# How a turned page is cut into four transfers on its way to DRAM: 128 partitions by 256 columns instead of 32 partitions by 1024 columns

## The chip, the cores and the metric

One core of one Trainium2 chip runs the whole kernel. A core has a matrix engine (TensorE, PE in the profile), a vector engine (VectorE, DVE), a scalar engine (ScalarE, ACT), a general engine (GpSimd, POOL), a sequencer that only issues transfers here (SyncE, SP), and 16 DMA engines that carry transfers between DRAM and the on-chip buffer (SBUF, 128 partitions). The metric is the device time of one execution in microseconds (us); lower is better. Changes of less than 0.2% are taken as no change.

## The reference, cut to what matters

Two layers of an encoder with 256 tokens of width 4096. Each layer normalises, multiplies by one wide weight matrix (4096 x 11264), runs 16 attention heads and 8 bidirectional retention heads on the pieces, and multiplies back by 4096 x 4096:

```python
for l in range(DEPTH):                       # DEPTH = 2
    proj = rmsnorm(x, norm_w[l]) @ w_in[l]
    aq, ak, av, ag, rq, rk, rv, rg = jnp.split(proj, SPLIT_POINTS, axis=-1)
    aq = apply_axial_rope(rmsnorm(aq...), rope) * attn_scale
    ak = apply_axial_rope(rmsnorm(ak...), rope)
    a_out = jax.nn.silu(ag) * gqa_attention(aq, ak, av)
    r = bidirectional_retention(rope(rq), rope(rk) * ret_scale, rv, ...)
    r_out = jax.nn.silu(rg) * rmsnorm(r, ret_norm[l])
    x = x + jnp.concatenate([a_out, r_out], axis=-1) @ w_out[l]
return rmsnorm(x, final_norm)
```

All in float32. The kernel gets that precision by splitting each operand into a high and a low part and summing three products on PE.

## The kernel before, in words

**Weights.** The two weight matrices stream from DRAM in tiles of 128 x 1024 elements (512 KB). SP loads most of them (`wraw`); ACT casts each to its high part (`whi`), DVE subtracts to get the low part (`wlo`). Some groups use a seven-product scheme, for which DVE also forms sums of tiles (`wsum`). Every few tiles are "far": POOL loads the high part directly (`fhi`), ACT writes its negative into `flo`, and POOL then issues a second load of the same weights that is added onto `flo`. PE multiplies `whi`, `wlo`, `fhi`, `flo` by the activations (`x7h`, `x7l`, `x8h`, `x8l`) into eight PSUM banks (`M` in the profile).

**Side work.** Beside this stream, the results of each block become rotary queries and keys, gates, attention probabilities and retention weights. Small products of these go through one PSUM bank (`ps`) at places that are fixed between the weight products of PE's program.

**Turning.** A product often needs its operand with tokens and features exchanged. That is done in two halves. `turned` is one DVE instruction that transposes each 32 x 32 block of a page of 128 x 1024 elements, in place among the partitions. `store` then writes the page to a DRAM buffer with the blocks exchanged, in four transfers of 128 KB that POOL issues one after the other. A later transfer (`fetch`, or `Turn.fetch`, or the two loads of `retention_weights`) reads the buffer back as a whole. `store` is called for the turned keys (`k_dram`), queries (`q_dram`), gates (`g_dram`), attention probabilities (`p_dram`), retention queries and keys (`rq_dram`, `rk_dram`) and for the activations of the next matrix (`next_dram`).

In the buffer, element (row 32b + e, column 256a + f) comes from the page's partition 32a + e, column 256b + f, with a and b from 0 to 3, e from 0 to 31 and f from 0 to 255. A contiguous piece is therefore 256 elements, 1 KB, and a store has 512 of them.

**Who waits.** A fetch waits for all four transfers of its store. The page itself lies in one of nine shared buffers (`pg`); whatever is written next into that buffer waits for the four transfers too.

**What sets the order.** A model in the kernel (classes `Model` and `Rings`) plays the program while it is written and decides, engine by engine, the order of the instructions; the result is a fixed program. The model prices a transfer by `transfer`, from the length of its contiguous piece and the number of pieces. All instructions are issued from one recording helper, so nearly all have the line L458 in the profile, and tile names tell them apart.

Of the kernel before, what the change touches and what calls it, by code (L numbers as in the profile page):

```python
# [19 lines left out]
SEQ = 256  # L20
# [13 lines left out]
BLK = 32  # L34
# [490 lines left out]
def hybrid_encoder(  # L525
# [14 lines left out]
    ve, ac, pe, gp, sy = (  # L540
        Engine(e, engine, model, active)
        for e, engine in (("V", nc.vector), ("A", nc.scalar), ("P", nc.tensor), ("G", nc.gpsimd), ("S", nc.sync))
    )
# [39 lines left out]
    def drop(n=1):  # L583

        def dropped():
            held[0] -= n
            own(-n)

        do(dropped)
# [839 lines left out]

    def store(room, to):  # L1430

        to = to.rearrange("(b e) (a f) -> a e b f", e=BLK, a=4)
        for a in range(4):
            gp.dma_start(to[a], room[BLK * a : BLK * (a + 1), :].rearrange("e (b f) -> e b f", b=4))
        drop()

    def fetch(src, name):
# [48 lines left out]
    def rotary(v, L, kind, to):  # L1486
# [38 lines left out]
        drop()  # L1525
        yield
        store(v, to)
        return rs if kind == "aq" else None

# [15 lines left out]
    def attention_pair(g, h, kv, qT, rs, done):  # L1545
# [38 lines left out]
        drop()  # L1584
        yield
        store(room, p_dram[2 * (g % 2) + h // 2])
        yield

# [26 lines left out]
    def attention_group(L, g, gacc, qacc):  # L1615
        def gates():
            yield from gate(gacc, L)
            room = page([P, KG * SEQ], "room")
            turned(gacc, room)
            drop()  # L1620
            yield
            store(room, g_dram[g % 2])

        yield from gates()
        while "aq" not in L.tables:
            yield
        rs = yield from rotary(qacc, L, "aq", q_dram[g % 2])
        yield
        L.rs[g] = rs
# [701 lines left out]
```

## Time and profile before

| | |
|---|---|
| median of 3 runs | 2576.78 us (2576.16 to 2577.53) |
| the profiled execution's own time | 2576.86 us |
| its span in the profile | 2575.1 us |
| PE busy | 2562.3 us |
| DVE busy | 2374.0 us |
| ACT busy | 1706.2 us |
| POOL busy | 459.7 us |
| granted PE clock | 0.999 |

The span runs from the first to the last instruction of the program; 1.8 us of the execution lie outside it. PE is busy nearly all the time, but its busy time is no proof that it never waits, so its waits are read apart. "A <- B" in a list of waits says that A stood idle until B was done, with the total in us, the number of times and the longest. In a timeline each row has the start, the length, the engine, the operation, the tiles written and read, and in brackets the idle time before and what ended it. "POOL DMA_DIRECT2D" is the time in which POOL issues a transfer, not the time until it has landed.

### The profile page before, as it was taken

What the parts mean: (1) busy time and instruction counts of PE and PEld (TensorE: products, weight loads), DVE (VectorE), ACT (ScalarE), POOL (GpSimd) and SP (SyncE); (2) the same over time, 40 slices, a digit from 0 to 9 for tenths busy, and PEclk for the clock granted to TensorE, in tenths of its full rate; (3) what the DMA queues carried; (4) which work ended last, traced back from release to release, by engine and by line L of the source; (5) the groups of instructions that cost most, each with busy time, mean ns of one, the idle gap of its engine ahead of it and who ended that gap; (6) DMA issues with size and microseconds to landing.
All of it is one profiled execution on the core that took longest, in us unless ns stands there. A gap on an engine that the chain in (4) does not pass through costs nothing.

```text
span 2575.1 us, 34335 instructions
## 1 busy us (share of the span) xinstructions
PE 2562.3 (100%) x11482; PEld 2120.2 (82%) x11482; DVE 2374.0 (92%) x3001; ACT 1706.2 (66%) x2459; POOL 459.7 (18%) x676
## 2 busy tenths in 40 slices
PE   9999999999999999999999999999999999999998
PEld 6888888888888888888888888888888888888886
DVE  7999999999989999988999999999999899999887
ACT  7866676666655668665776666766666566776565
POOL 0111221211111111111221112212211112111111
PEclk9999999999999999999999999999999999999999
DMA  8988988988778787988998989888887887888986
GB/s 316 316 266 267 290 258 275 287 273 254 224 238 260 227 288 239 295 263 254 331 310 253 274 260 297 275 262 285 272 264 233 241 250 234 284 248 265 270 255 219
DMA packets 197969, 687.07 MB, mean 267 GB/s; under 512 B 24224, under 2 KB 24352, under 8 KB 197792
## 3 DMA queue, kind: packets, MB, share of 16 engines
q1 hardware_dynamic: 126592, 446.81, 49.1%
q0 software_dynamic: 71200, 238.07, 36.8%
q8 instruction: 90, 1.47, 0.2%
q14 instruction: 87, 0.71, 0.1%
HBM read 637.60 MB, written 47.19 MB: 266 GB/s over the span
## 4 chain that ended last, share of the span: by engine, by line
PE 98%; DMA 1%; DVE 0%; issue 0%; ACT 0%; POOL 0%; SPq 0%; POOLq 0%; DVEq 0%; ACTq 0%
PE M L458 94%; PE ps L458 4%; DMA q<-q_dram 0%; DMA full<-in_xT 0%; DVE wlo L458 0%; ACT full L458 0%; DVE cb L458 0%; SPq L458 0%; ACT whi L458 0%; ACT x7h L458 0%; DVE xf L458 0%; ACT pTh L458 0%; POOL last L458 0%; ACT ps L458 0%; DVE aql L458 0%
## 5 line engine op out<-in xcount | busy, mean ns | idle before, releaser
L458 ACT CAST whi<-wraw 128x1024 fp32r<-128x1024 f32 (+1 forms) x814 | 757.2, 936 | 336.0 <-PE M L458 289.8
L458 DVE TENSOR_TENSOR wlo<-wraw,whi 128x1024 fp32r<-128x1024 f32 (+1 forms) x814 | 869.6, 1077 | 47.5 <-ACT whi L458 43.8
L458 ACT CAST whi<-wsum 128x1024 fp32r<-128x1024 f32 x416 | 436.7, 1050 | 264.5 <-PE M L458 121.7
L458 DVE TENSOR_TENSOR wlo<-wsum,whi 128x1024 fp32r<-128x1024 f32 x416 | 507.3, 1220 | 91.1 <-ACT whi L458 61.1
L458 PE MATMUL M<-whi,x7h 128*128 128x512 f32 x1463 | 569.9, 390 | 0.0
L458 PE MATMUL M<-whi,x7l 128*128 128x512 f32 x1463 | 569.6, 389 | 0.0
L458 PE MATMUL M<-wlo,x7h 128*128 128x512 f32 x1463 | 475.0, 389 | 0.0
L458 PE MATMUL M<-whi,x8l 128*128 128x512 f32 x1165 | 453.6, 389 | 0.0
L458 PE MATMUL M<-whi,x8h 128*128 128x512 f32 x1165 | 453.6, 389 | 0.0
L458 PE MATMUL M<-wlo,x8h 128*128 128x512 f32 x1165 | 361.1, 389 | 0.0
L458 PEld LDWEIGHTS M<-wlo,x7h 128*128 128x128 f32 x1463 | 274.5, 188 | 57.6 <-DVE wlo L458 0.4
L458 PEld LDWEIGHTS M<-whi,x7h 128*128 128x128 f32 x1463 | 274.7, 188 | 56.8 <-DVE cb L458 0.4
L458 PEld LDWEIGHTS M<-whi,x7l 128*128 128x128 f32 x1463 | 274.7, 188 | 56.4 <-issue 0.2
L458 DVE TENSOR_TENSOR wsum<-wraw 128x1024 f32<-128x1024 f32 x208 | 253.6, 1219 | 4.2 <-DMA wraw<-in_w_out 1.6
L458 PEld LDWEIGHTS M<-wlo,x8h 128*128 128x128 f32 x1165 | 218.7, 188 | 45.6
L458 PEld LDWEIGHTS M<-whi,x8h 128*128 128x128 f32 x1165 | 218.7, 188 | 45.5 <-DVE ca L458 0.6
L458 PEld LDWEIGHTS M<-whi,x8l 128*128 128x128 f32 x1165 | 218.7, 188 | 45.3 <-DVE x8l L458 0.3
L458 ACT ACTIVATE flo<-fhi 128x1024 fp32r<-128x1024 f32 (+1 forms) x142 | 149.1, 1050 | 143.0 <-PE M L458 140.9
L458 PE MATMUL M<-whi,x 128*128 128x512 f32 x738 | 227.4, 389 | 0.0
L458 POOL DMA_DIRECT2D fhi<-in_w_in x104 | 58.0, 557 | 863.0 <-PE M L458 852.7
L458 PE MATMUL M<-fhi,x8l 128*128 128x512 f32 x417 | 162.4, 389 | 0.0
L458 PE MATMUL M<-fhi,x8h 128*128 128x512 f32 x417 | 162.3, 389 | 0.0
(287 smaller groups left out, 3197.9 us busy)
## 6 DMA issues: line engine op xcount, KB each, us to landing
wraw<-in_w_in SPq DMA_DIRECT2D x596, 512.0 KB, 5.7
wraw<-in_w_out SPq DMA_DIRECT2D x218, 512.0 KB, 6.1
fhi<-in_w_in POOLq DMA_DIRECT2D x104, 512.0 KB, 4.8
flo<-in_w_in POOLq DMA_DIRECT2D x104, 512.0 KB, 8.2
fhi<-in_w_out POOLq DMA_DIRECT2D x35, 512.0 KB, 4.8
flo<-in_w_out POOLq DMA_DIRECT2D x35, 512.0 KB, 8.5
full<-next_dram POOLq DMA_DIRECT2D x24, 512.0 KB, 8.7
p_dram<-room POOLq DMA_DIRECT2D x64, 128.0 KB, 5.3
```

The costliest lines, as they stand in the source:

```text
L458: op.call()
```

## The change

`store` still makes four transfers of 128 KB to the same places. Before, each took 32 partitions of the page with all their 1024 columns; now each takes all 128 partitions with 256 columns. The walk on the DRAM side was 32 rows (4 KB apart), in each of them four pieces 128 KB apart; now it is four pieces of a row (1 KB apart), for each of them 32 rows 4 KB apart.

```diff
     def store(room, to):
 
-        to = to.rearrange("(b e) (a f) -> a e b f", e=BLK, a=4)
-        for a in range(4):
-            gp.dma_start(to[a], room[BLK * a : BLK * (a + 1), :].rearrange("e (b f) -> e b f", b=4))
+        to = to.rearrange("(b e) (a f) -> b a e f", e=BLK, a=4)
+        for b in range(4):
+            gp.dma_start(to[b], room[:, b * SEQ : (b + 1) * SEQ])
         drop()
```

Piece length and piece count are the same (128 pieces of 1 KB in a transfer), so the model's price is the same, and every engine's instructions stand in the same order as before. Only the shape of the stores differs, in every one of them. Two places on POOL show it, with the shape on the DRAM side at the end of a row. The first is in layer 0, a store of turned queries and one of attention probabilities, and the fetch of these (before, then now):

```order
L458 DMA q_dram<-cb 32x4x256 x4
L458 DMA p_dram<-room 32x4x256 x2
L458 DMA fhi<-in_w_in 128x1024
L458 DMA p_dram<-room 32x4x256
L458 DMA flo<-in_w_in 128x1024
L458 DMA p_dram<-room 32x4x256
L458 DMA pT<-p_dram 128x1024
```

```order
L458 DMA q_dram<-cb 4x32x256 x4
L458 DMA p_dram<-room 4x32x256 x2
L458 DMA fhi<-in_w_in 128x1024
L458 DMA p_dram<-room 4x32x256
L458 DMA flo<-in_w_in 128x1024
L458 DMA p_dram<-room 4x32x256
L458 DMA pT<-p_dram 128x1024
```

Nothing moved; the transfers of a store count 4 x 32 rows of 256 elements instead of 32 x 4. The second is in layer 1, two stores of attention probabilities with the weight loads and the fetches around them (before, then now):

```order
L458 DMA p_dram<-room 32x4x256 x3
L458 DMA fhi<-in_w_in 128x1024
L458 DMA p_dram<-room 32x4x256
L458 DMA flo<-in_w_in 128x1024
L458 DMA sgT<-g_dram 128x1024
L458 DMA pT<-p_dram 128x1024
L458 DMA p_dram<-room 32x4x256 x4
```

```order
L458 DMA p_dram<-room 4x32x256 x3
L458 DMA fhi<-in_w_in 128x1024
L458 DMA p_dram<-room 4x32x256
L458 DMA flo<-in_w_in 128x1024
L458 DMA sgT<-g_dram 128x1024
L458 DMA pT<-p_dram 128x1024
L458 DMA p_dram<-room 4x32x256 x4
```

Here too a weight load stands between the third and the fourth transfer of a store, as before.

## The prediction

> **What bounds the kernel now.** I read the page's busy times first, then the list of PE's waits, since a busy PE alone proves nothing.
>
> ```profile
> span 2575.1 us, 34335 instructions
> PE 2562.3 (100%) x11482; PEld 2120.2 (82%) x11482; DVE 2374.0 (92%) x3001; ACT 1706.2 (66%) x2459; POOL 459.7 (18%) x676
> ...
> PE ps L458 <- DVE junk L458: 1.1, 1, 1.1
> PE M L458 <- DMA fhi<-in_w_in: 1.0, 2, 0.7
> PE M L458 <- ACT full L458: 0.2, 1, 0.2
> ```
>
> PE is the bound: it lacks 12.8 us of the span, and its waits on others sum to 2.3 us. The only wait on a transfer is 1.0 us, on a weight load. So no store of a turned page costs PE a visible moment today. A faster store can therefore give back 1.0 us at the very most, while a slower one can cost, if somewhere the slack between a store's landing and PE is thin. That asymmetry decides the forecast, so the rest of the reading is about slack. First the transfers themselves, from the list of issues, the queues, and the view of the tile `room`:
>
> ```profile
> q1 hardware_dynamic: 126592, 446.81, 49.1%
> q0 software_dynamic: 71200, 238.07, 36.8%
> p_dram<-room POOLq DMA_DIRECT2D x64, 128.0 KB, 5.3
> next_dram<-room POOLq DMA_DIRECT2D x64, 128.0 KB, 6.5
> L458 POOL DMA_DIRECT2D p_dram<-room x64: 552/574/912, 255.8 to 1835.1; - x64
> DMA to landing us min/median/max: 2.4/5.5/11.8
> DMA packets 197969, 687.07 MB, mean 267 GB/s; under 512 B 24224, under 2 KB 24352, under 8 KB 197792
> ```
>
> POOL's queue is q0, SP's is q1. Only 128 packets lie between 512 B and 2 KB, so the 1 KB pieces of the stores (512 in a page) do not travel as packets of their own; four share one of 4 KB. A transfer of a store takes POOL 0.574 us to issue and lands 2.4 us later when nothing is in its way, 5.5 us in the middle, 11.8 us at worst.
>
> Then who stands still until a store has landed, from the waits of POOL and of DVE:
>
> ```profile
> POOL pT L458 <- DMA p_dram<-room: 35.1, 5, 11.5
> POOL full L458 <- DMA next_dram<-room: 21.9, 4, 9.4
> POOL rkq L458 <- DMA rq_dram<-cb: 11.2, 3, 5.2
> POOL k L458 <- DMA k_dram<-ca: 5.9, 1, 5.9
> DVE pTl L458 <- DMA p_dram<-room: 1.8, 2, 1.1
> ```
>
> Thirteen times POOL holds a fetch, and all that is queued behind it, until the last transfer of a store is in. Twice DVE itself stops, because `pTl` is written into the buffer that a store is still reading. DVE is 92% busy, so time that it loses is not soon made up.
>
> **The change, part by part.**
>
> *POOL's instructions.* Four issues per store stay four, in the same order, with the same waits that matter. Their length should stay 0.574 us, since the pieces are as many (128). Should it depend on pieces per DMA engine instead, the nearest longer issue is that of `rkq`:
>
> ```profile
> L458 POOL DMA_DIRECT2D rkq<-rk_dram x8: 884/916/1067, 599.1 to 2149.5; - x8
> ```
>
> That is 0.34 us more, 1.0 us over the three issues ahead of a store's last. I take nothing, since the count of pieces is nearest to the store's own row, and keep 1.0 us for the upper end.
>
> *What carries a transfer.* Before, both sides of a transfer count 32 rows outermost; now the page's side counts 128 and the DRAM side 4. If the work is handed to DMA engines along the outermost count, a transfer that was spread over sixteen can now go to four. From q0's row: 36.8% of 16 x 2575.1 us is 15,162 us of engine time for 238.07 MB, so a packet of 4 KB takes 0.261 us. A transfer is 32 packets. On sixteen engines that is two each, 0.52 us; on four it is eight each, 2.09 us. No row decides between the two: no transfer of before has an outermost count so small. I hold four the likelier, because four rows to hand out cannot occupy sixteen engines unless the walk is cut through its second dimension as well.
>
> The Trainium skill, page "DMA: Bandwidth & Descriptors", section "Why a DMA increments its semaphore by 16 and not by 1", says that a transfer runs on the largest number of engines up to 16 that divides the slowest size of both sides. By that rule it is 16 before (32 and 32) and 4 now (4 and 128), and the sum below holds; with sixteen it would be 2576.9 us. No run here shows it yet.
>
> *How much later the last transfer of a store lands.* If each transfer takes a different quarter of the engines, an engine carries eight packets per store as before, but the quarter of the last transfer starts only with the last issue. On an empty queue the last lands 2.09 - 0.52 = 1.57 us later. Where SP's loads take every second turn, packets last twice as long and the store is bound by its eight packets: before they begin with the first issue, now with the last, and the four issues span 2.22 us (row below), so 2.22 - 0.56 = 1.66 us. Where other loads of POOL are already queued on all engines, nothing changes. So 0 to 1.66 us; I use 1.6 where the queue was free and less where it was not.
>
> *Place A, 1833 to 1862 us (layer 1).*
>
> ```profile
> 1833.44 2.22 POOL L458 DMA_DIRECT2D p_dram<-room  x4 [4.37 <-DVE room L458]
> 1841.04 1.23 DVE L458 TENSOR_TENSOR pTl<-pT,pTh 128x1024 fp32r<-128x1024 f32 x1 [1.05 <-DMA p_dram<-room]
> 1841.00:1862.00 21.00, 21.00 (x94) 17.17 (x92) 20.92 (x27) 12.82 (x16) 4.58 (x8) 1.00 0.87 254
> 1860.75 1.22 DVE L458 TENSOR_TENSOR pTl<-pT,pTh 128x1024 fp32r<-128x1024 f32 x1
> 1862.07 0.46 PE L458 MATMUL ps<-pTl,kv 128*128 128x512 f32 x1
> ```
>
> DVE waits for the store, then works 20.92 of the next 21.00 us without a gap up to the second `pTl`, which ends at 1861.97; PE uses it at 1862.07. Slack 0.10 us. Cost 1.6 - 0.1 = **1.5 us** (0 to 1.6).
>
> *Place B, 557 to 616 us (layer 0).*
>
> ```profile
> 557.36 2.22 POOL L458 DMA_DIRECT2D p_dram<-room  x4 [6.36 <-DVE wlo L458]
> 565.27 1.23 DVE L458 TENSOR_TENSOR pTl<-pT,pTh 128x1024 fp32r<-128x1024 f32 x1 [0.72 <-DMA p_dram<-room]
> 604.30 1.23 DVE L458 TENSOR_TENSOR wlo<-wsum,whi 128x1024 fp32r<-128x1024 f32 x1 [0.59 <-ACT whi L458]
> 615.67 0.68 DVE L458 TENSOR_TENSOR cb<-cb,M 128x512 f32<-128x512 f32 x1
> 616.41 0.50 PE L458 MATMUL M<-whi,x7h 128*128 128x512 f32 x1
> ```
>
> The same wait, and at the far end PE starts on a bank 0.06 us after DVE has emptied it (615.67 + 0.68 = 616.35). In between DVE has idle time, 0.59 us in the row shown, that could absorb half. Cost **0.8 us** (0 to 1.6).
>
> *Place C, 387 to 428 us (layer 0).*
>
> ```profile
> 387.89 0.91 POOL L458 DMA_DIRECT2D p_dram<-room  x1
> 400.27 0.56 POOL L458 DMA_DIRECT2D pT<-p_dram  x1 [11.46 <-DMA p_dram<-room]
> 413.07 0.55 POOL L458 DMA_DIRECT2D next_dram<-sgT  x1 [7.81 <-DVE sgT L458]
> 414.18 0.54 POOL L458 DMA_DIRECT2D q<-q_dram  x1
> 424.92 0.62 ACT L458 CAST aqh<-q 128x512 fp32r<-128x512 f32 x1 [1.43 <-DMA q<-q_dram]
> 427.67 1.29 DVE L458 TENSOR_TENSOR aql<-q,aqh 128x512 fp32r<-128x512 f32 x2
> 428.41 0.39 PE L458 MATMUL ps<-kv,aql 128*128 128x256 f32 x1
> ```
>
> Every step waits for the one before, from the store through `pT` and `sgT` to the next queries; the first of the two `aql` ends half way through its 1.29 us, at about 428.3, and PE uses it at 428.41. But this store landed some 12 us after its last issue (387.89 to 400.27) where the least is 2.4, so its queue was full and the delay is nearer to 0 than to 1.6. Cost **0.6 us** (0 to 1.6).
>
> *Weight loads queued behind a store.* They share q0, and on the last quarter of the engines they now find more packets ahead. `flo` at 826.46 us follows a store:
>
> ```profile
> 826.46 0.90 POOL L458 DMA_DIRECT2D flo<-in_w_in  x1 [1.43 <-ACT flo L458]
> 836.91 0.61 PE L458 MATMUL M<-flo,x8h 128*128 128x512 f32 x2
> DMA to landing us min/median/max: 4.1/8.2/12.9
> ```
>
> PE needs it 10.4 us after its issue, while landings of `flo` reach from 4.1 over 8.2 to 12.9 us. Only the late tail has no slack. I take three loads with half a microsecond each, **1.5 us** (0 to 5).
>
> *The other twelve waits of POOL* (thirteen less place C). Passed on whole they would cost 12 x 1.6 = 19 us; but today's 74 us of such waits reach PE nowhere, so the truth is near the low end: **1.5 us** (0 to 6).
>
> Sum: 1.5 + 0.8 + 0.6 + 1.5 + 1.5 = 5.9 us. The profiled execution took 2576.86 us, 1.8 us more than its span and 0.08 us above the median of the runs; with 5.9 us it comes to 2582.8. Upper end: 1.6 + 1.6 + 1.6 + 5 + 6 = 15.8 us, 2592.7; the 1.0 us of longer issues would bring no more than it has room for.
>
> **Rivals.**
>
> *The stores are still carried by sixteen engines, or their delay is covered* (not slower). Then nothing changes that PE sees: 2576.9 us, give or take 0.7 as the runs do. For it: PE waits for no store today, and the pieces are the same. Against it: slacks of 0.10 and 0.06 us at A and B.
>
> *All four transfers go to the same four engines.* Then a store is 32 packets on each, 8.4 us instead of 2.1, and its last lands 6.3 us later on an empty queue and twice that beside SP's loads. It decides from about 3 us on, where the twelve other waits lose their slack too. A, B and C cost 6 each, half of the other twelve waits 6 each (36), loads behind stores some 25: about 80 us, 2657. For it: nothing in the trace forbids it. Against it: every transfer would have to begin with the same engine.
>
> The same section of the Trainium skill says that such a transfer takes consecutive engines from a cursor that goes round. By that, four transfers would fill all sixteen, which speaks against this rival; no row here shows it.
>
> *The stores land earlier.* Neighbouring pieces now go to rows 4 KB apart instead of 128 KB, which could shorten writes. PE could gain its 1.0 us of waiting: 2575.9. More than 0.2% (5.2 us, about what can be told from no change) is out of reach, as PE's waits hold only 2.3 us.
>
> **How the numbers follow.** Forecast 0.62, sixteen engines or covered 0.27, one quarter 0.08, earlier landing 0.03. Inside the forecast the cost lies above 5.2 us in about three cases of four, as the terms are skewed upward. Slower: 0.62 x 0.75 + 0.08 = 0.55; same 0.62 x 0.25 + 0.27 = 0.42; faster 0.03, kept for what I have not seen. The range takes in the second case below (2576.0) and the upper end of the forecast above (2593.0); the one-quarter case is left out. The forecast's own range is 2578 to 2593.
>
> **What would show it.** Four engines: the least landing of a store rises from 2.4 to about 4 us, with q0's packets still 71200. Place A: DVE's wait for `p_dram<-room` grows from 1.8 us, and `ps` appears among PE's waits near 1862 us. Loads: `flo` appears among PE's waits. If the least landing stays at 2.4, the second case holds, and I was wrong on the engines; if landings grow by 1.6 and PE still waits for nothing, I was wrong on the slack.

## The result and the profile after

The changed kernel took 2613.09 us (median of 4 runs, 2607.07 to 2614.9), the kernel before 2577.16 us beside it (2576.16 to 2580.39): a ratio of 1.0133, 95% interval 1.0114 to 1.0152, so 29 to 39 us slower. The forecast was 2582.8 us and its range ended at 2593.0: the direction was right, the size six times too small. The profiled execution took 2607.07 us, its span 2605.3, which is 30.2 us more than the span before. From its page:

```profile
span 2605.3 us, 34340 instructions
...
PE 2574.2 (99%) x11482; PEld 2121.7 (81%) x11482; DVE 2373.0 (91%) x3001; ACT 1700.3 (65%) x2459; POOL 489.7 (19%) x676
...
DMA packets 220241, 687.43 MB, mean 264 GB/s; under 512 B 46496, under 2 KB 46624, under 8 KB 220064
...
q1 hardware_dynamic: 126592, 446.81, 47.4%
q0 software_dynamic: 93472, 238.42, 37.3%
```

Two things stand out. POOL's queue q0 carries 22,272 packets more than before, all under 512 B, and only 0.35 MB more. That is 96 for each of the 232 store transfers, 16 bytes each. Eight data packets on each of four engines and eight padding packets on each of the twelve others make just this count (12 x 8). So a transfer does run on four engines, but the others are not left alone. The other thing is PE: its busy time grew by 11.9 us, although it does the same work, and its waits by the rest of the 30.2 us. The longest of PE's waits:

```profile
PE M L458 <- DMA flo<-in_w_in: 8.5, 5, 3.0
PE M L458 <- DVE ca L458: 2.9, 2, 2.7
PE ps L458 <- DVE aql L458: 2.6, 2, 1.5
PE M L458 <- ACT whi L458: 2.0, 3, 1.1
PE ps L458 <- DVE junk L458: 1.1, 1, 1.1
PE ps L458 <- DVE pTl L458: 1.1, 3, 0.6
PE M L458 <- DVE wlo L458: 1.1, 2, 0.5
```

Before, no wait on `flo` stood there at all; now it is the longest. The view of `room` and the waits of POOL and DVE say what became of the stores:

```profile
L458 POOL DMA_DIRECT2D p_dram<-room x64: 667/690/1059, 258.4 to 1862.6; - x64
DMA to landing us min/median/max: 3.9/7.8/14.8
```

```profile
POOL pT L458 <- DMA p_dram<-room: 45.6, 6, 14.6
POOL full L458 <- DMA next_dram<-room: 27.8, 4, 10.5
POOL rkq L458 <- DMA rq_dram<-cb: 23.9, 4, 8.3
POOL k L458 <- DMA k_dram<-ca: 10.9, 2, 7.7
DVE pTl L458 <- DMA p_dram<-room: 4.8, 2, 2.9
```

An issue of the attention stores takes 0.690 us in place of 0.574. The least landing rose from 2.4 to 3.9 us, which is the 1.5 us of the forecast, but the median rose by 2.3 and the latest by 3.0. From the issue and landing records of all 58 stores of the two profiled executions, in us after each transfer's own issue (means):

| transfer of a store | 1 | 2 | 3 | 4 | first to fourth issue |
|---|---|---|---|---|---|
| before | 4.64 | 5.12 | 6.04 | 6.47 | 2.03 |
| after | 6.21 | 7.45 | 8.47 | 9.21 | 2.44 |

The fourth lands 2.74 us later after its issue, and its issue comes 0.41 us later: a store is complete 3.15 us later, where the forecast had 1.6. The delay also grows from transfer to transfer (1.57, 2.33, 2.43, 2.74), and nothing in the forecast made it grow, since each of the four has a quarter of the engines to itself.

### The profile page after: what moved, and what is told of

Its sections match the earlier page's. It is cut to its first block, busy times and chain, and to the rows that moved or that the text cites. A ratio compares the mean times of both kernels' runs of the same rounds, so it can differ in the third digit from the quotient of the medians.

```text
span 2605.3 us, 34340 instructions
## 1 busy us (share of the span) xinstructions
PE 2574.2 (99%) x11482; PEld 2121.7 (81%) x11482; DVE 2373.0 (91%) x3001; ACT 1700.3 (65%) x2459; POOL 489.7 (19%) x676
## 2 busy tenths in 40 slices
DMA packets 220241, 687.43 MB, mean 264 GB/s; under 512 B 46496, under 2 KB 46624, under 8 KB 220064
## 4 chain that ended last, share of the span: by engine, by line
PE 77%; DMA 5%; issue 3%; DVE 3%; POOL 2%; ACT 1%; DVEq 0%; POOLq 0%; ACTq 0%
PE M L458 74%; PE ps L458 3%; DMA flo<-in_w_in 2%; DMA p_dram<-room 2%; DVE wlo L458 1%; DMA q<-q_dram 1%; DVE wsum L458 1%; ACT whi L458 0%; POOL p_dram L458 0%; DMA wraw<-in_w_in 0%; DMA pT<-p_dram 0%; ACT pr L458 0%; DVE cb L458 0%; DVE room L458 0%; DVE rot L458 0%
```

## The experiments

All times are medians in us; the kernel before took 2576 to 2577 in every group, and a ratio is against it.

**The engine count alone.** The page's side stays 128 by 256; the DRAM side is counted in another way, over the same 128 KB, with every engine's order as in the changed kernel. What it leaves out is the exchange of the blocks, so its result is not the reference's; the same holds for every run below whose edit has `(j g f)`, but for the small transfers beside the old stores:

```diff
-        to = to.rearrange("(b e) (a f) -> b a e f", e=BLK, a=4)
+        to = to.rearrange("(b e) f -> b (e f)", e=BLK)
         for b in range(4):
-            gp.dma_start(to[b], room[:, b * SEQ : (b + 1) * SEQ])
+            gp.dma_start(to[b].rearrange("(j g f) -> g j f", g=16, f=SEQ), room[:, b * SEQ : (b + 1) * SEQ])
```

> The page's side keeps 128 partitions by 256 columns and the same contiguous 128 KB of the buffer; only the DRAM side of each transfer is counted as 16 x 8 pieces instead of 4 x 32, so the pieces land permuted inside their 128 KB (the blocks are not exchanged as the reference needs). Engines and padding theories: sixteen engines carry each transfer, packets under 512 B fall from 46496 back to 24224, the least landing of an attention store from 3.9 to about 2.4 us, time 2577 us, give or take 3. Shape theory (the 128 by 256 cut itself is slow, whatever the engines): 2605 to 2615 us.

With `g=8` in the same place:

> As the run before, with the DRAM side counted as 8 x 16 pieces (again permuted inside their 128 KB). Engines theory: eight engines with four data packets each; packets under 512 B 24224 + 232 transfers x 8 idle engines x 4 = 31648; time 2578 to 2581 us. Padding theory (each small packet takes a turn beside SP's packets): the same count, time 2580 to 2590. Shape theory: about 2613.

With `g=2`:

> As the runs with 16 x 8 and 8 x 16 pieces on the DRAM side, now 2 x 64: two engines, sixteen data packets each (the pieces again permuted inside their 128 KB). Packets under 512 B: 24224 + 232 x 14 x 16 = 76192. Engines theory: 2625 to 2640 us. Padding theory: 2650 to 2680.

| outermost count of the DRAM side | 16 | 8 | 4 (the change) | 2 |
|---|---|---|---|---|
| time | 2576.04 | 2580.2 | 2613.09 | 2759.55 |
| ratio | 0.9997 (0.9988 to 1.0007) | 1.0014 (1.0004 to 1.0023) | 1.0133 (1.0114 to 1.0152) | 1.0706 (1.069 to 1.0722) |

The view of `room` and the packets with 16:

```profile
L458 POOL DMA_DIRECT2D p_dram<-room x64: 532/542/857, 254.4 to 1834.1; - x64
DMA to landing us min/median/max: 2.3/5.3/11.5
```

```profile
DMA packets 197969, 687.07 MB, mean 267 GB/s; under 512 B 24224, under 2 KB 24352, under 8 KB 197792
```

Nothing is lost with sixteen. So the cut into 128 partitions by 256 columns costs nothing by itself, and the theory of the shape falls; all of the loss goes with the outermost count of 4. With 8 the time lies in the ranges of both other theories, so it does not part them. The packet counts came as forecast for 8 (31,648) and for 2:

```profile
DMA packets 249937, 687.90 MB, mean 250 GB/s; under 512 B 76192, under 2 KB 76320, under 8 KB 249760
```

```profile
PE M L458 <- DMA flo<-in_w_in: 55.2, 16, 7.4
```

With 2 the time lay far beyond both theories (2625 to 2640, and 2650 to 2680). But here something is at work that the change does not have. In the view of `room`, POOL stands still before 60 of the transfers, without a cause that the profile names, 226.5 us in all; in the changed kernel it is 0.7 us:

```profile
  issue: 226.5, 60
```

The fourth transfer of a store is issued 8.50 us after the first (mean), where it is 1.99 us with sixteen engines. So the run with 2 does not show how the loss of the change grows with the engines' load.

**A mark on the transfer.**

```diff
-            gp.dma_start(to[b], room[:, b * SEQ : (b + 1) * SEQ])
+            gp.dma_start(to[b], room[:, b * SEQ : (b + 1) * SEQ], single_packet=True)
```

> The stores of the changed kernel, with each transfer marked as a single packet. Padding theory: the idle engines' share goes as one turn in place of eight, so the time falls to 2580 to 2595 us. Engines theory (only the concentration on four engines counts): 2600 us or more. The packet counts say whether the mark changed anything.

It took 2608.05 (ratio 1.0124, 1.0109 to 1.0139), and its packets are the same to the last one (220241, under 512 B 46496). The mark changed neither packets nor, clear of the noise, the time, so the run tells no theory from another. It is one more sample of the changed kernel: 31.6 us over the kernel before in its own group, where the first was 35.9 us over, hence the 31 to 36 us from here on.

**Telling the planner.**

```diff
-    return max(1.0, math.prod(out.shape) / n) / 16 * each, each, adding
+    return max(1.0, math.prod(out.shape) / n) / max(v for v in range(1, 17) if out.shape[0] % v == 0 == src.shape[0] % v) * each, each, adding
```

> The stores of the changed kernel, but the planner prices a transfer by the engines that carry it (four for a store, in place of sixteen), so it moves other work around the stores. Slack theory (PE waits because the fixed order leaves no slack for the later landing): most of the 36 us comes back, under 2590 us. If the loss is bandwidth of the queue that no order can hide: about 2613.

And the same order with the stores of the kernel before:

> The order that the planner makes when it prices the stores at four engines (the run of that name, 2635 us), but with the stores of the kernel before, on sixteen engines. If that order is simply a worse one: 2590 to 2610 us, above the 2577 of the kernel before by most of the 22 us that the repriced plan lost. If the order is as good as the old one and the later landings cost more in it: 2575 to 2582.

Both forecasts failed, the second narrowly. The repriced plan took 2635.43 with the new stores (1.0227, 1.0208 to 1.0245) and 2613.63 with the old ones (1.014, 1.0125 to 1.0155). The new order is worse by 36 us by itself, and the stores cost 22 us in it, less than the 36 us in the old order. So this planner does not find an order that is good in all. Why the stores cost less in it is not shown: it may give them more slack, or its other waits may hide theirs. In it PE waits for the tail of the attention whichever stores it has, 12.9 us with the new ones and with the old stores:

```profile
PE ps L458 <- DVE pTl L458: 10.0, 4, 4.3
```

**Small transfers beside the old stores.** Each of the four old transfers is followed by one of 2 KB:

```diff
+            gp.dma_start(extra[a].rearrange("(j g f) -> g j f", g=16, f=4), room[:, a * SEQ : a * SEQ + 4])
```

> The stores of the kernel before, and behind each of their transfers one more of 2 KB (128 pieces of 16 B, written to a buffer that nobody reads), whose DRAM side counts 16 x 8 pieces: sixteen engines. It is the control of the next run. Four more issues per store (232 x 0.55 = 128 us of POOL) and another order of the program: 2577 to 2610 us by either theory. Packets under 512 B: 24224 + 232 x 32 = 31648, if four pieces share a packet as in the stores.

With `g=4`:

> As the run before, in the same order on every engine, but the DRAM side of the 2 KB transfers counts 4 x 32 pieces: four engines have data, the other twelve only padding. The 128 KB transfers keep their sixteen engines, so no data worth a name is concentrated. Padding theory (each small packet takes a turn of the queue): 31648 + 232 x 96 = 53920 packets under 512 B, and the time 8 to 25 us above the control, most of the 36 us of the change. Engines theory (only the data on four engines counts): within 4 us of the control.

2597.09 (1.0075, 1.006 to 1.009) and 2601.86 (1.0089, 1.0072 to 1.0106): 4.8 us apart, with overlapping intervals. The pair missed its aim, as the packets of the second run show, 30,720 where 53,920 were expected:

```profile
DMA packets 205395, 687.93 MB, mean 265 GB/s; under 512 B 30720, under 2 KB 31776, under 8 KB 205216
```

In the packet records an engine with data has one packet of 512 B (32 pieces of 16 B in one), and each of the twelve others one of 128 B. So a padding packet is there for each data packet, not for each piece, and here it is only one; in it lie 4 bytes for every piece of an engine with data (32 x 4 = 128 here, and 4 x 4 = 16 in the change). The pieces are as many as in the change, though: 128 with data and, at 4 bytes each, 384 of padding. And the 128 KB transfers beside them landed no later, 6.26 us after their issue in the mean (6.30 in the control). So that many padding pieces, in few packets, do not delay a store. What is left to cost time is mainly the length of the issue. The view by tile, `g=16` and then `g=4`:

```profile
L458 POOL DMA_DIRECT2D extra_dram<-room x160: 533/541/915, 191.1 to 2296.4; - x160
```

```profile
L458 POOL DMA_DIRECT2D extra_dram<-room x160: 682/700/1071, 190.8 to 2302.4; - x160
```

0.16 us more on each of 232 issues cost 4.8 us at most. In the change an issue is longer by 0.12 us, so this is likely no more than a few of its 31 to 36 us.

**The stores on SP's queue.** In both, `sy.dma_start` takes the place of `gp.dma_start`; the control keeps the old cut, the other has the new one.

> The stores of the kernel before, issued by SP in place of POOL; the planner makes another order. It is the control of the next run. Without a forecast of its own beyond 2570 to 2640 us, since weight loads then queue behind stores; packets under 512 B may change with the queue.

> The stores of the changed kernel, issued by SP, in the same order as the run before. If SP's queue also hands a transfer to four engines and pads the rest: 22272 more packets under 512 B than in the control, and 20 to 60 us more. If it hands it to four engines without padding, the difference to the control is the engines theory alone: 5 to 15 us. If it spreads the 128 rows of the page over sixteen engines whatever the DRAM side counts: no more packets, within 3 us of the control; then the loss belongs to POOL's queue.

2585.3 (1.0028, 1.0017 to 1.0039) and 2694.54 (1.0456, 1.044 to 1.0471): 109 us apart, which none of the three cases held. The packets of the control and of the new cut:

```profile
DMA packets 220243, 687.08 MB, mean 265 GB/s; under 512 B 24225, under 2 KB 54049, under 8 KB 220065
```

```profile
DMA packets 217459, 687.07 MB, mean 255 GB/s; under 512 B 21441, under 2 KB 51265, under 8 KB 217281
```

SP's queue pads nothing: 2784 = 232 x 12 packets are gone, those by which the twelve other engines closed a transfer. But here the four transfers of a store all go to the same four engines: the packet records show mostly four 1 KB packets in flight and hardly ever more than five, and a store takes 8.9 us (median) from its first packet to the end of its last, where the control has up to sixteen or a few more in flight and takes 5.1. That is the forecast's second rival, on another queue; it was priced at 80 us. The Trainium skill, page "DMA: Bandwidth & Descriptors", section "Why a DMA increments its semaphore by 16 and not by 1", on which the forecast drew for its four engines, has both queues so: the lowest-numbered engines for SP, a cursor that goes round for POOL. The traces agree as far as they show it, in the packet counts of all four outermost counts too. As a test of padding against concentration the pair is void, since it concentrates four times as much.

**Which stores carry the loss.** The new cut for one group of stores, the old one for the rest:

```diff
+        name = to[:, :].tensor.name
+        if name[0] == "p":
+            to = to.rearrange("(b e) (a f) -> b a e f", e=BLK, a=4)
...
+        else:
+            to = to.rearrange("(b e) (a f) -> a e b f", e=BLK, a=4)
```

> Only the stores of the attention probabilities (64 of 232 transfers) are cut as in the changed kernel, all others as before. 64 x 96 = 6144 more packets under 512 B, 30368 in all. If the cost falls by number of transfers: 28% of the 36 us, 2587. If it falls mainly where attention stores stand among weight loads (places A and B, and the loads of flo that PE waited for): 2590 to 2597. If the change's cost comes from stores that gather at the same time: under 2582.

With `name.startswith("next")`:

> Only the stores for the next matrix (64 of 232 transfers) are cut as in the changed kernel. 30368 packets under 512 B. By number of transfers 2587. If the attention stores carry the cost: 2578 to 2582, and the two runs together leave about 10 to 15 of the 36 us for the queries, keys, gates and retention.

With all but these two groups:

> The complement of the two runs before: queries, keys, gates and the retention's stores (104 of 232 transfers) are cut as in the changed kernel, attention probabilities and the next matrix's pages as before. 24224 + 104 x 96 = 34208 packets under 512 B. If the costs of the three groups add up, the rest of the 31 to 36 us lies here: 2597 to 2602. If the groups amplify each other (a delay of one meets a slack that another has used up): 2580 to 2590, and the three single costs sum to 15 to 25 us.

| stores with the new cut | transfers | time | ratio |
|---|---|---|---|
| attention probabilities | 64 | 2584.02 | 1.0027 (1.0018 to 1.0036) |
| pages of the next matrix | 64 | 2581.97 | 1.002 (1.0011 to 1.003) |
| queries, keys, gates, retention | 104 | 2590.32 | 1.0059 (1.0038 to 1.008) |

7, 5 and 14 us, 26 in all, against 31 to 36 for all together. The first lay between two of its forecasts (under 2582, and 2587), the second in the range for the case that the attention stores carry the cost, which the first denies. The last run's share lay between its two forecasts. With these intervals the loss mostly adds up; that the groups also amplify each other is likely but not shown. The attention stores, on which the forecast put its places A and B, carry only about a fifth.

**Half the data per transfer.** Eight transfers of 64 KB, with 16 and then with 4 as the DRAM side's outermost count:

```diff
+        to = to.rearrange("(b e) f -> b (e f)", e=BLK // 2)
+        for b in range(8):
+            gp.dma_start(to[b].rearrange("(j g f) -> g j f", g=16, f=SEQ // 2), room[:, b * SEQ // 2 : (b + 1) * SEQ // 2])
```

> Control of the next run: a store in eight transfers of 128 partitions by 128 columns (64 KB), the DRAM side counted as 16 x 8 pieces of 512 B (permuted inside their 64 KB): sixteen engines. Twice as many issues (232 x 0.55 = 128 us more of POOL) and another order: 2580 to 2610 us. Packets under 512 B: 24224 and 232 x 16 = 3712 more that close a transfer, 27936.

> As the control, in the same order, but the DRAM side counted as 4 x 32 pieces: four engines with four data packets each, in place of eight in the changed kernel; 464 transfers x 12 x 4 = 22272 small packets, as many as in the changed kernel. Engines theory: the data of the last transfer keeps its four engines half as long, so the loss is half of the changed kernel's or less, 5 to 17 us over the control. Padding theory: the turns in the queue are as many as before (32 per engine and store against 8), 20 us or more over the control.

2595.28 (1.0072, 1.0057 to 1.0088) and 2613.11 (1.0145, 1.012 to 1.0171): 18 us apart, right between the two forecasts. The packets are as forecast (50,208 under 512 B). It does not decide between the theories.

**A quarter of the pieces.** A store in four transfers of 32 partitions by 1024 columns, so pieces of 4 KB; the data, the engines and the packets stay those of the change:

```diff
+        to = to.rearrange("(b e) f -> b (e f)", e=BLK)
         for b in range(4):
+            gp.dma_start(to[b].rearrange("(j g f) -> g j f", g=4, f=4 * SEQ), room[BLK * b : BLK * (b + 1), :])
```

Its control has `g=16`.

> Control of the next run: a store in four transfers of 32 partitions by 1024 columns whose DRAM side is 16 x 2 pieces of 4 KB (a plain copy of the page, the blocks not exchanged): sixteen engines, 32 pieces per transfer in place of 128. Slightly another order. 2570 to 2600 us; packets under 512 B 24224.

> As the control, in the same order, but the DRAM side counts 4 x 8 pieces of 4 KB: four engines with eight data packets each, as in the changed kernel, and 12 x 8 = 96 small packets per transfer, again 46496 under 512 B; but each small packet now stands for one piece in place of four (96 padding pieces in place of 384). Padding theory by packets, and engines theory: no change, 25 to 40 us over the control. If the pieces are what costs (POOL's queue must write a padding piece for each data piece, 512 per transfer in all): most of it gone, under 15 us over the control.

2583.85 (1.0033, 1.002 to 1.0046) and 2588.89 (1.0053, 1.0036 to 1.007): 5 us apart in place of 36. The packets of the second are those of the change, to the last small one, and its stores land earlier:

```profile
DMA packets 220241, 687.16 MB, mean 266 GB/s; under 512 B 46496, under 2 KB 46624, under 8 KB 220064
```

```profile
L458 POOL DMA_DIRECT2D p_dram<-room x64: 562/584/929, 251.2 to 1847.6; - x64
DMA to landing us min/median/max: 3.2/6.4/12.6
```

Its control, with sixteen engines:

```profile
DMA to landing us min/median/max: 2.2/5.5/9.8
```

So eight data packets on each of four engines, with 96 small packets on the others, cost 5 us in this order, which is not quite the order of the change. Neither the concentration nor the number of small packets makes the 31 to 36 us alone; most of it goes with the 1 KB pieces. Against the change, this pair has both a quarter of the padding pieces (96 per transfer in place of 384) and a quarter of the data pieces on each of the four engines (8 in place of 32), so it does not tell these two apart. At sixteen engines the length of the pieces makes little difference: a store is complete 8.4 us after its first issue with 4 KB pieces and 8.3 us with 1 KB.

## Why the prediction was right in direction and wrong in size

Pairs with one order on every engine can be put side by side, by how much later a store's last transfer lands (measured from the store's first issue, mean over 58 stores, from the records) and by what the time lost. The pairs with 4 KB pieces, with eight transfers and with the repriced plan each have an order of their own; the others share the order of the change:

| pair | store complete later by | loss |
|---|---|---|
| outermost count 8 against 16 | 1.26 us | 4 us |
| 4 KB pieces, 4 against 16 | 1.41 us | 5 us |
| eight transfers, 4 against 16 | 2.77 us | 18 us |
| repriced plan, new stores against old | 3.14 us | 22 us |
| change against before | 3.15 us | 36 us |
| change against outermost count 16 | 3.40 us | 37 us |
| outermost count 2 against 16 | 8.3 us | 184 us |

In the order of the change, 1.26 us cost 4 us and 3.40 us cost 37, so the slack is used up somewhere between; the last row has POOL's standing still in it and is another case. At about 1.3 to 1.4 us the losses are 4 and 5 us, and the forecast's 5.9 us for its 1.6 us fits that in size. So the forecast's reading of the slack was about right as a sum, though not place by place, and the step that failed is "How much later the last transfer of a store lands": "0 to 1.66 us", and 3.15 us measured. The term of its sum that grew most by it is "Weight loads queued behind a store": 1.5 us, and 8.5 us measured. By its own steps:

*Four engines* was right: the least landing rose from 2.4 to 3.9 us, and the count of 16 took all of the loss away. "With q0's packets still 71200" was wrong: 22,272 padding packets came on top.

That the least landing rose by just the 1.5 us of the forecast is in part luck. With 4 KB pieces and the same four engines it rose by 1.0 us (2.2 to 3.2), which is what six more packets make by estimate at 0.159 us, the commonest length of a 4 KB packet on q0; the forecast's 0.261 us is a mean beside other traffic.

*The last transfer.* The concentration on four engines gave about what was forecast for it, 1.6 us: the pair with 4 KB pieces has it, with all the packets, and measured 1.41. What was missing comes with the 1 KB pieces on four engines: 3.40 less 1.41 leaves 2.0 us for the pieces and their longer issue. How the pieces cost this time is open. The engines do not spend it on padding packets: one of 16 bytes takes 11 ns (median of the packet records), so the eight of a transfer keep an idle engine busy for 0.09 us. That POOL's queue takes longer to write 512 pieces than 128 has one store for it, where SP's queue was quiet (issues at 693.03, 693.79 and 694.47 us): the first padding packets of the second transfer came 1.45 us after those of the first, though the issues are 0.75 us apart, and on q0 only the first transfer's packets were in flight between. Against a plain price per piece stand the small transfers, with as many pieces and no later landing beside them, and the run of eight transfers, with twice the pieces per store and only 2.77 us.

*POOL's issues* were taken at nothing with 1.0 us as the upper end for three issues; they take 0.12 us more each, and the fourth came 0.41 us later, on top of the landing.

*Place A* was sized right: DVE waits 2.95 us for the store where it waited 1.05, PE loses 0.65 us at `ps`, and from 1871 to 1891 us it falls 1.5 us further behind its old times (forecast 1.5). *Place B* cost little: DVE's wait grew from 0.72 to 1.82 us, and DVE had made up 0.65 us of that by 614 us. PE does wait 2.74 us there, at a product 1.4 us ahead of the one that the forecast names, but not for that store. The chain goes back through DVE to ACT, which waits for a weight load of SP's (`wraw`, issued at 607.22 us): it landed after 10.42 us where it took 8.14. From the timelines, the third line of the kernel before, the others of the changed kernel:

```profile
572.85 1.23 DVE L458 TENSOR_TENSOR pTl<-pT,pTh 128x1024 fp32r<-128x1024 f32 x1 [1.82 <-DMA p_dram<-room]
617.74 1.05 ACT L458 CAST whi<-wraw 128x1024 fp32r<-128x1024 f32 x1 [4.01 <-DMA wraw<-in_w_in]
607.90 1.05 ACT L458 CAST whi<-wraw 128x1024 fp32r<-128x1024 f32 x1 [0.71 <-DMA wraw<-in_w_in]
624.34 0.47 PE L458 MATMUL M<-whi,x7h 128*128 128x512 f32 x1 [2.74 <-DVE ca L458]
1870.01 1.23 DVE L458 TENSOR_TENSOR pTl<-pT,pTh 128x1024 fp32r<-128x1024 f32 x1 [2.95 <-DMA p_dram<-room]
1890.98 0.51 PE L458 MATMUL ps<-pTl,kv 128*128 128x512 f32 x1 [0.65 <-DVE pTl L458]
```

A store of retention queries is under way then. With the new cut on the queries, keys, gates and retention alone the same load takes 9.99 us and PE waits 1.71 us there; with it on the attention stores alone, 8.36 and 0.94. With the outermost count of 16, where nothing is lost, it is 9.15 and 0.78, so a part of this comes and goes from run to run. The forecast had no term for SP's loads beside a store.

*Weight loads queued behind a store* is the term that was mis-sized most: 1.5 us (0 to 5), and 8.5 us of waits measured. The five loads landed 1.5 to 4.4 us later after their issue than before. The load that the forecast named is one of them; its 10.4 us from issue to use were short by 2.0:

```profile
837.46 0.88 POOL L458 DMA_DIRECT2D flo<-in_w_in  x1 [1.39 <-ACT flo L458]
850.02 0.72 PE L458 MATMUL M<-flo,x8h 128*128 128x512 f32 x2 [2.02 <-DMA flo<-in_w_in]
```

*Place C* has no wait of PE near 428 us that is longer than before, but its store did cost: `pT` came late, ACT cast it late, and PE waited 1.10 us for the `whi` behind it at 412.11 us (forecast 0.6, by another path). *The other twelve waits* (1.5 us, 0 to 6) show in PE's waits on `aql`, 2.6 us behind late fetches of `q`, and in 0.75 us on a `whi` behind another `pT`. The chains of the 1.1 us on `wlo` lead back to no store.

*Not forecast at all* was, beside SP's loads, that PE goes slower after a long wait, of which the last section tells. Of the 11.9 us by which its busy time grew, this explains some 5; the rest is spread thin over the first products after its waits and isn't explained further.

## What to carry to other kernels

Before a transfer is cut another way, count the outermost size on both sides: at 4 in place of 16 this one lost its engines, and on POOL's queue every piece brought three padding pieces on the idle ones. Ask also how long the pieces are: with 4 KB pieces four engines cost 5 us here, with 1 KB pieces 31 to 36. When work stands in a fixed order, ask how late a transfer may come before PE feels it, and expect a steep rise behind that point: here 1.3 us cost 4 us, and 3.2 us cost 36. A price given to the planner must be tried with the old transfers too, since a new order can cost as much as the change that it was meant to absorb.

## What the hardware showed that was not expected

The padding stands above. The issue itself follows the engine count at equal data and pieces: 0.542 us on sixteen engines, 0.613 on eight, 0.690 on four and 0.805 on two (medians of the attention stores).

And PE, after some waits of about 2 us and more, runs at half pace for a while. In the timeline of the changed kernel, and in its table of stretches (the granted clock stands after POOL's figures, then the DMA share and GB/s):

```profile
1359.38 1.22 PE L458 MATMUL M<-flo,x8h 128*128 128x512 f32 x2 [3.00 <-DMA flo<-in_w_in]
1360.40 0.63 PE L458 MATMUL M<-flo,x 128*128 128x512 f32 x1
...
1362.11 0.63 PE L458 MATMUL M<-wlo,x7h 128*128 128x512 f32 x1
1362.54 0.48 PE L458 MATMUL M<-whi,x7h 128*128 128x512 f32 x1
...
1363.09 0.39 PE L458 MATMUL M<-whi,x7h 128*128 128x512 f32 x1
1363.32 0.40 PE L458 MATMUL M<-whi,x7l 128*128 128x512 f32 x1
```

```profile
1355.00:1364.00 9.00, 6.00 (x20) 4.50 (x19) 8.60 (x15) 7.27 (x13) 1.40 (x2) 0.81 0.87 323
1366.00:1376.00 10.00, 10.00 (x45) 8.28 (x45) 9.90 (x16) 7.96 (x15) 0.00 (x0) 1.00 0.61 187
```

Products start 0.43 us apart where they started 0.23 apart before and after, and the clock of the stretch is 0.81. The clock's records show half speed for 3.41 us at three places, near 625, 850 and 1359 us, each behind one of the three longest waits; each costs 1.7 us. So each of these waits cost PE more than half as much again. It does not follow every such wait: in the run with the new cut on the queries, keys, gates and retention, PE waited 2.42 us at 156 us and went on at full clock:

```profile
156.38 0.50 PE L458 MATMUL M<-flo,x8h 128*128 128x512 f32 x1 [2.42 <-DMA flo<-in_w_in]
154.00:164.00 10.00, 7.62 (x33) 6.30 (x34) 9.12 (x18) 6.71 (x11) 2.13 (x3) 1.00 0.90 253
```

The Trainium skill, page "TensorE: Matmul & The Clock Gate", section "What's actually happening", gives one idle window of about 3.4 us as what lowers the clock; in the changed kernel waits of 2.02, 2.74 and 3.00 us, all shorter, went with it.
